# A decoder block's FFN down projection: deeper operand look-ahead, another order of its seven products, and a last product that is finished group by group

## The chip, the cores and the metric

The kernel runs on one core of a Trainium2 chip. The metric is the device time of one execution in microseconds (us); the time given for a kernel is the median of its runs.

A core has these engines, each with a queue of its own that is worked off in order: PE (matrix products, into PSUM), DVE (elementwise vector work), ACT (copies, casts, activations), POOL (here a power of small columns) and SP, which in this kernel issues all DMAs. Engines wait for each other by semaphores.

## The reference

One decoder block on x of 2048 tokens by 1024, all in float32, batch 1. The first half (attention and mLSTM mixers) is not touched. The change is in the feed-forward half:

```python
h2 = modulate(rms_norm(x, g_pre_ffn[l]), shift_f, scale_f)
ff = (jax.nn.silu(h2 @ w_ffn_gate[l]) * (h2 @ w_ffn_up[l])) @ w_ffn_down[l]
x = x + gate_f[:, None, :] * rms_norm(ff, g_post_ffn[l])
```

w_ffn_gate and w_ffn_up are 1024 x 2816, w_ffn_down is 2816 x 1024. The last product, its root-mean-square norm over 1024 columns and the residual sum are what the text below calls "down".

## The kernel before

A float32 product is made of three PE products of split operands: each operand is cast by ACT to a high half (fp32r) and DVE subtracts that from the original for the low half; high x high, high x low and low x high are summed in PSUM. Such a pair of halves for a 128 x 512 operand is a tile called `hl`; a ring of four `hl` tiles is shared by all of this (an operand part of down needs two: one of the activations, one of the weight).

The FFN is the second program of the kernel, `program2`. It works on two blocks of 1024 tokens: gate_up(0), down(0), gate_up(1), down(1). gate_up and down use a scheme of seven products in place of eight for a product of 2 x 2 quadrants. `PROD` names the operands of the seven, activation first: 11·11, 12·21, S2·T2, 22·T4, S1·T1, S3·T3, S4·22 (the S and T are sums of quadrants). Products 1, 3, 5 and 7 (index in `IN_X` = 0, 2, 4, 6) add up in one set of four PSUM tiles, `acc`, that is never cleared within a stage; products 2, 4 and 6 go to a second set of four, `mix`. The four tiles of a set are the four groups of 128 tokens.

In down(b2) a product has 11 parts along the contraction (2816 / 2 / 128), and a part is for each of the four token groups three matmuls of 512 columns: 7 x 11 x 4 x 3 = 924 matmuls of a stage.

- `load_ab` loads two parts at once, 1 MB, from the DRAM scratch `as_d` (sums of activations that gate_up stored, L1472) and from `ws_d` or w_ffn_down (L1475, L1478). Its tile is a `raw` (a pool of two) or a `big` (a pool of nine), as `raw2` counts; every second one is a `big` when `F["deep"]` is set.
- `run2` drives it: up to two loads are alive at a time, four when deep, and the operands of up to `ahead` parts (2 in down) are split (`split_unit`, L1146 on ACT, L1147 on DVE) before the part's matmuls are written.
- At the end of each product `combine` reads the PSUM tiles: after products 1, 3 and 5 a copy on ACT, after 2 and 4 one sum on DVE per token group, after 6 two sums (L1375, L1376), which complete quadrants 21 and 22. With quadrant 11 complete after product 2, 21 and 22 after 6, 12 after 7, `done` runs a chain for each token group: square and row sum on ACT (L1492), multiplication by the gain on DVE (L1494), and where both halves of a row are there the sum (L1499), the mean (L473, DVE), a power -1/2 (L476, POOL), and two scalar_tensor_tensor on DVE (L1506) with the loaded x1 rows, each followed by a store to the output.
- In down(0), seven of the nine `big` tiles hold gate_up(1)'s operands of h (`HC`), until gate_up(1) ends. The same stage also makes the next block's h by a stream, `h_combine`: x1 loads (`ob`), DVE L1245, four transposes on PE (L210), ACT L1253, and its splits and sums. A stream's steps are written between matmuls of products in `acc` only, by `tick`, where its own clock of modelled time says so.

The order in which each engine runs its instructions is set by a scheduler at build time, from the program order, the dependencies and its own costs, unless instructions are kept in program order by hand. Of the DMA semaphores eight take turns, so that a DMA may wait for the one eight before.

## Time and profile before

| quantity | value |
|---|---|
| median of 3 runs | 2745.63 us (2745.53 to 2746.5) |
| profiled execution | 2749.36 us, its span 2747.7 us |
| PE busy | 2688.8 us, 98% |
| DVE busy | 1927.2 us, 70% |
| ACT busy | 1235.1 us, 45% |
| granted clock, mean | 0.993 |
| down(0) by the trace | 1868.07 to 2098.12 us |
| gate_up(1) | to 2516.8 us |
| down(1), PE's part | to 2736.3 us |

The profile is that of one execution. Times are us from the span's start. "L1147" is a line of the kernel, "hl<-big,hl" the output tile and the inputs by their names in the program, "x4" a number of instructions in a row, and a bracket such as "[1.81 <-DVE hl L1147]" says that the engine stood idle for 1.81 us before and what ended the wait. PE's duration of one matmul (0.39 us) is longer than the distance between starts, since matmuls overlap.

### The profile page before, as it was taken

Reading aid. Unit: us, or ns where it says so; the run is one execution under the profiler, and the core shown is the slowest. Engines: PE = TensorE matmul, PEld = TensorE weight load, DVE = VectorE, ACT = ScalarE, POOL = GpSimd, SP = SyncE. Lnnn points to the kernel's source line nnn. Section 1 sums busy time; section 2 is a strip of 40 time slices with the busy share of each in tenths; the row PEclk is TensorE's granted clock in tenths of the full one; section 3 lists DMA queues with packets and bytes.
Section 4 is the critical chain, followed back from the end, with each engine's and each line's share of the span. In section 5 each row is a group of like instructions: output and inputs, shape, how many; then the busy total and the mean of one; then the engine's idle time right before and its main releaser. Section 6 shows DMA issues by size and latency. Waiting matters only on the chain.

```text
span 2747.7 us, 35099 instructions
## 1 busy us (share of the span) xinstructions
PE 2688.8 (98%) x12654; PEld 2203.2 (80%) x12654; DVE 1927.2 (70%) x3780; ACT 1235.1 (45%) x2278; POOL 238.0 (9%) x255
## 2 busy tenths in 40 slices
PE   6999999999999999999999999999999999999997
PEld 4778887788887887878887888887877888888886
DVE  7768657677776876668747777776669666666556
ACT  4543354533555345564334333334555333333444
POOL 3100121001211012110111000000001000000000
PEclk8999999999999999999999999999999999999999
DMA  7233254252453534434457444456557332326534
GB/s 230 94 113 99 92 177 131 81 154 93 149 158 105 167 116 161 163 106 147 140 201 262 152 154 173 142 188 211 199 201 248 114 102 98 111 96 238 209 132 169
DMA packets 282102, 417.32 MB, mean 152 GB/s; under 512 B 18996, under 2 KB 176312, under 8 KB 280136
## 3 DMA queue, kind: packets, MB, share of 16 engines
q1 hardware_dynamic: 281928, 415.08, 45.6%
q8 instruction: 99, 1.62, 0.2%
q14 instruction: 75, 0.61, 0.1%
HBM read 331.11 MB, written 83.92 MB: 151 GB/s over the span
## 4 chain that ended last, share of the span: by engine, by line
PE 86%; DVE 6%; DMA 4%; ACT 2%; issue 1%; SPq 0%; POOL 0%; POOLq 0%; DVEq 0%; ACTq 0%
PE acc L205 60%; PE mix L205 24%; PE mix L210 2%; DVE tm L427 1%; DMA tx<-in_x_dram 1%; DMA ob<-x 1%; DMA hc_d<-os 1%; DVE hl L1147 1%; DMA tx<-in_w_ada_dram 1%; DMA big<-in_x_dram 0%; DVE wlo L263 0%; DMA big<-in_w_ada_dram 0%; ACT hl L1146 0%; DMA w<-x 0%; ACT whi L262 0%
## 5 line engine op out<-in xcount | busy, mean ns | idle before, releaser
L262 ACT CAST whi<-raw 128x1024 fp32r<-128x1024 f32 (+1 forms) x208 | 211.8, 1019 | 425.4 <-PE acc L205 349.9
L263 DVE TENSOR_TENSOR wlo<-raw,whi 128x1024 fp32r<-128x1024 f32 (+1 forms) x208 | 252.8, 1216 | 144.6 <-ACT whi L262 142.3
L205 PE MATMUL acc<-hhi,wlo 128*128 128x512 f32 x896 | 353.9, 395 | 0.0
L205 PE MATMUL acc<-hlo,whi 128*128 128x512 f32 x896 | 352.4, 393 | 0.0
L205 PE MATMUL acc<-hhi,whi 128*128 128x512 f32 x896 | 352.1, 393 | 0.2 <-ACT whi L262 0.2
L1146 ACT CAST hl<-raw 128x512 fp32r<-128x512 f32 x309 | 185.0, 621 | 224.9 <-PE mix L205 127.6
L205 PE MATMUL acc<-hl,hl 128*128 128x512 f32 x1056 | 252.1, 396 | 8.4 <-DVE hl L1147 6.9
L205 PE MATMUL acc<-big,hl 128*128 128x512 f32 x1056 | 253.9, 389 | 0.3 <-ACT w L1368 0.3
L1147 DVE TENSOR_TENSOR hl<-raw,hl 128x512 fp32r<-128x512 f32 x309 | 206.9, 687 | 67.3 <-ACT hl L1146 65.1
L205 PEld LDWEIGHTS acc<-hl,hl 128*128 128x128 f32 x1056 | 198.4, 190 | 55.2 <-DVE hl L1147 12.2
L205 PEld LDWEIGHTS acc<-big,hl 128*128 128x128 f32 x1056 | 198.1, 188 | 41.7 <-ACT w L1368 0.7
L1147 DVE TENSOR_TENSOR hl<-big,hl 128x512 fp32r<-128x512 f32 x219 | 144.7, 687 | 84.5 <-ACT hl L1146 84.5
L1146 ACT CAST hl<-big 128x512 fp32r<-128x512 f32 x219 | 128.5, 621 | 159.2 <-PE acc L205 79.5
L205 PEld LDWEIGHTS acc<-hhi,wlo 128*128 128x128 f32 x896 | 168.4, 188 | 36.9 <-DVE tm L868 1.6
L205 PEld LDWEIGHTS acc<-hlo,whi 128*128 128x128 f32 x896 | 168.3, 188 | 36.6 <-issue 1.6
L205 PEld LDWEIGHTS acc<-hhi,whi 128*128 128x128 f32 x896 | 168.4, 188 | 34.4 <-ACT whi L262 0.6
L205 PE MATMUL mix<-big,hl 128*128 128x512 f32 x704 | 195.6, 389 | 0.0
L205 PE MATMUL mix<-hl,hl 128*128 128x512 f32 x792 | 181.1, 389 | 0.3 <-ACT hl L1146 0.3
L205 PEld LDWEIGHTS mix<-hl,hl 128*128 128x128 f32 x792 | 148.5, 188 | 31.9 <-ACT hl L1146 1.2
L205 PE MATMUL acc<-whi,big 128*128 128x512 f32 x512 | 164.7, 395 | 1.4 <-ACT whi L262 1.4
L205 PE MATMUL acc<-big,whi 128*128 128x512 f32 x512 | 157.6, 392 | 0.0
L205 PEld LDWEIGHTS mix<-big,hl 128*128 128x128 f32 x704 | 132.1, 188 | 27.4
(309 smaller groups left out, 5113.8 us busy)
## 6 DMA issues: line engine op xcount, KB each, us to landing
raw<-in_w_in_dram SPq DMA_DIRECT2D x76, 1024.0 KB
as_d<-w SPq DMA_DIRECT2D x154, 256.0 KB
raw<-in_w_ffn_up_dram SPq DMA_DIRECT2D x22, 1024.0 KB
big<-as_d SPq DMA_DIRECT2D x41, 512.0 KB
tx<-in_w_ada_dram SPq DMA_DIRECT2D x64, 256.0 KB
raw<-in_w_out_dram SPq DMA_DIRECT2D x16, 1024.0 KB
raw<-as_d SPq DMA_DIRECT2D x29, 512.0 KB
hc_d<-os SPq DMA_DIRECT2D x28, 512.0 KB
```

The source lines that it names most:

```text
L205: return T.matmul(o, lhsT=lhsT, rhs=rhs, start=start, stop=stop, skip_group_check=resumed)
L210: T.transpose(o, i, ident[:k, :k])
L262: A.copy(hv, src)
L263: eng.tensor_tensor(lv, src, hv.bitcast(F32), op=ALU.subtract)
L427: V.scalar_tensor_tensor(acc, raw[:, k, :], c_, acc, op0=ALU.mult, op1=ALU.add)
L1146: A.copy(v(hi), src)
L1147: V.tensor_tensor(v(lo), src, v(hi).bitcast(F32), op=ALU.subtract)
```

## The change

- The order of the products is 1, 4, 3, 6, 5, 2, 7 (index 0, 3, 2, 5, 4, 1, 6), and `gather` stands in place of `combine` in down: quadrant 21 is complete after product 6, the fourth to run, 22 after product 5, 11 after product 2, the sixth, and 12 last. The copies and sums of a stage are as many as before.
- `ahead` is 3 in down(0) and 4 in down(1). One part of three in down(0), and two of four in down(1), are split into a `big` tile ("roomy") in place of two `hl`.
- `F["deep"]` is a number: 2 at first, 3 from the last pair of gate_up(0) on, 4 from the end of down(0) on. That many loads are alive; with 3 every third load is a `big`, with 4 every second.
- The last four parts of product 7 in down(1) (`HELD`) are kept in four `big` tiles. Their 48 matmuls come at the end, one token group after the other, 12 for each, pinned in program order.
- `done` became a generator `chain`. In down(0) and for quadrant 12 it runs on the spot; for the other quadrants of down(1) it is run as a stream, `after`, behind the sums, and is finished ahead of the held parts.

```diff
-                if nload < len(raws) and alive < (4 if F["deep"] else 2):
+                if nload < len(raws) and alive < F["deep"]:
...
-        return big(shape) if F["deep"] and F["loads"] % 2 else raw_tile(shape)
+        return big(shape) if F["deep"] > 2 and F["loads"] % (2 if F["deep"] == 4 else 3) == 1 else raw_tile(shape)
...
+        def done(t):
+            def go(qd, y, in_psum):
+                steps = chain(t, qd, y, in_psum)
+                if in_psum:
+                    next(steps)
+                if in_psum or not last:
+                    for _ in steps:
+                        pass
+                else:
+                    behind.append(steps)
...
+        def after():
+            while True:
+                while behind:
+                    yield from behind.pop(0)
+                if F["chained"] == b2:
+                    return
+                yield 1000.0
...
+        def gather(i, ps, r, done):
+            if i == 0:
+                r["P1"] = unit()
+                A.copy(r["P1"], ps)
+            elif i == 3:
+                r["Q"] = unit()
+                A.copy(r["Q"], ps)
+            elif i == 2:
+                V.tensor_tensor(r["Q"], ps, r["Q"], op=ALU.add)
+            elif i == 5:
+                r["Z"] = unit()
+                A.copy(r["Z"], ps)
+                V.tensor_tensor(r["Q"], ps, r["Q"], op=ALU.add)
+                done("21", r["Q"], False)
+            elif i == 4:
+                V.tensor_tensor(r["Z"], ps, r["Z"], op=ALU.add)
+                done("22", r["Z"], False)
+            elif i == 1:
+                V.tensor_tensor(r["P1"], ps, r["P1"], op=ALU.add)
+                done("11", r["P1"], False)
+            else:
+                done("12", ps, True)
+
+        ahead = 4 if last else 3
...
         def make(raw, i, p, j):
+            roomy = made[0] % ahead in ((0, 2) if last else (0,))
+            made[0] += 1
+            held = last and i == 6 and p >= NP - HELD
+
             def prep():
+                if held or roomy:
+                    t = big([4, TB], F32R)
+                    return split_unit(raw.tile[:, j, :], t[:, 0, :], t[:, 1, :]) + split_unit(raw.tile[:, 2 + j, :], t[:, 2, :], t[:, 3, :])
                 return split_unit(raw.tile[:, j, :]) + split_unit(raw.tile[:, 2 + j, :])
...
+                if held:
+                    if not kept:
+                        F["chained"] = b2
+                        finish([F["after"]])
+                    kept.append(ab)
+                    if p < NP - 1:
+                        return
...
+                pin = tc.keep_in_program_order if held else lambda ins: ins
...
+                    for ah, al, bh, bl in kept if held else [ab]:
+                        pin(mm(ps, ah[:, c], bh, p == 0 and i in (0, 1, 3, 5), False, True))
+                        pin(mm(ps, ah[:, c], bl, False, False, True))
+                        pin(mm(ps, al[:, c], bh, False, p == NP - 1 and ah is ab[0], True))
...
-            pt.ahead = 2
+            pt.ahead = HELD if held else ahead
...
-        for i in range(7):
+        for i in (0, 3, 2, 5, 4, 1, 6):
```

How the instructions stand on the engines, at three places. In these rows a name carries two numbers, the tile's and the buffer's count, and rows with the same names are put together as "x3".

PE where gate_up(0) ends and down(0) begins, before: `big` operands with `acc2747` are gate_up's last parts, `acc2768` to `acc2770` belong to down's first part, and `ob2780` is what the stream transposes.

```order
L205 MATMUL acc2747_16216<-big2231_12755,hl2749_16231 128x512
L205 MATMUL acc2747_16216<-big2230_12753,hl2749_16231 128x512
L205 MATMUL acc2768_16375<-hl2761_16339,hl2760_16336 128x512
L205 MATMUL acc2769_16376<-hl2761_16339,hl2760_16336 128x512
L205 MATMUL acc2770_16377<-hl2761_16339,hl2760_16336 128x512
L205 MATMUL acc2768_16375<-hl2761_16339,hl2760_16336 128x512 x2
L205 MATMUL acc2769_16376<-hl2761_16339,hl2760_16336 128x512 x2
L205 MATMUL acc2770_16377<-hl2761_16339,hl2760_16336 128x512 x2
L210 MATMUL mix2788_16491<-ident_116,ob2780_16437 128x128 x4
L205 MATMUL acc2747_16216<-big2271_13032,hl2753_16269 128x512
```

The same place now:

```order
L205 MATMUL acc2747_16216<-big2230_12753,hl2749_16231 128x512
L210 MATMUL mix2787_16494<-ident_116,ob2779_16438 128x128 x4
L205 MATMUL acc2747_16216<-big2271_13032,hl2753_16269 128x512
L205 MATMUL acc2747_16216<-big2272_13034,hl2753_16269 128x512
L205 MATMUL acc2747_16216<-big2271_13032,hl2753_16269 128x512 x2
L205 MATMUL acc2747_16216<-big2272_13034,hl2753_16269 128x512
L205 MATMUL acc2747_16216<-big2271_13032,hl2753_16269 128x512 x2
L205 MATMUL acc2747_16216<-big2272_13034,hl2753_16269 128x512
L205 MATMUL acc2747_16216<-big2271_13032,hl2753_16269 128x512 x2
L205 MATMUL acc2747_16216<-big2272_13034,hl2753_16269 128x512
L205 MATMUL acc2747_16216<-big2271_13032,hl2753_16269 128x512
L205 MATMUL acc2768_16377<-big2758_16314 128x512
```

The nine matmuls of down's first part moved behind the transposes and gate_up's last part; that part's operands are now in a `big` tile, `big2758`.

DVE in down(1) where the sixth product to run ends, before: `mix3735` and the next three are that product's PSUM tiles, `w` the quadrants' sums, and L1147 the splits of coming parts.

```order
L1147 TENSOR_TENSOR hl3763_22811<-big3748_22694,hl3763_22811 128x512
L1375 TENSOR_TENSOR w3664_22141<-mix3735_22615,w3664_22141 128x512
L1376 TENSOR_TENSOR w3728_22589<-mix3735_22615,w3728_22589 128x512
L1375 TENSOR_TENSOR w3665_22146<-mix3736_22616,w3665_22146 128x512
L1376 TENSOR_TENSOR w3729_22594<-mix3736_22616,w3729_22594 128x512
L1375 TENSOR_TENSOR w3666_22151<-mix3737_22617,w3666_22151 128x512
L1376 TENSOR_TENSOR w3730_22599<-mix3737_22617,w3730_22599 128x512
L1375 TENSOR_TENSOR w3667_22156<-mix3738_22618,w3667_22156 128x512
L1376 TENSOR_TENSOR w3731_22604<-mix3738_22618,w3731_22604 128x512
L1147 TENSOR_TENSOR hl3796_22918<-big3748_22694,hl3796_22918 128x512
```

And now, after the sixth product to run (product 2):

```order
L1147 TENSOR_TENSOR big3746_22928<-raw3720_22763,big3746_22928 128x512
L1553 TENSOR_TENSOR w3564_21659<-mix3685_22581,w3564_21659 128x512
L1147 TENSOR_TENSOR big3747_22945<-raw3720_22763,big3747_22945 128x512
L1147 TENSOR_TENSOR big3748_22962<-big3729_22814,big3748_22962 128x512
L1553 TENSOR_TENSOR w3565_21664<-mix3686_22582,w3565_21664 128x512
L1147 TENSOR_TENSOR big3748_22962<-big3729_22814,big3748_22962 128x512
L1553 TENSOR_TENSOR w3566_21669<-mix3687_22583,w3566_21669 128x512
L1147 TENSOR_TENSOR big3749_22979<-big3729_22814,big3749_22979 128x512
L1553 TENSOR_TENSOR w3567_21674<-mix3688_22584,w3567_21674 128x512
L1147 TENSOR_TENSOR big3749_22979<-big3729_22814,big3749_22979 128x512
```

The eight sums in a row became four, with splits of parts far ahead (`big3746` to `big3749`, which hold the last parts of the last product) between them.

PE's last matmuls before, the last part of the last product:

```order
L205 MATMUL acc3563_21475<-hl3817_23089,hl3816_23086 128x512
L205 MATMUL acc3564_21476<-hl3817_23089,hl3816_23086 128x512
L205 MATMUL acc3565_21477<-hl3817_23089,hl3816_23086 128x512
L205 MATMUL acc3566_21478<-hl3817_23089,hl3816_23086 128x512
L205 MATMUL acc3563_21475<-hl3817_23089,hl3816_23086 128x512 x2
L205 MATMUL acc3564_21476<-hl3817_23089,hl3816_23086 128x512 x2
L205 MATMUL acc3565_21477<-hl3817_23089,hl3816_23086 128x512 x2
L205 MATMUL acc3566_21478<-hl3817_23089,hl3816_23086 128x512 x2
```

And now, from the second token group on:

```order
L205 MATMUL acc3541_21463<-big3749_22979 128x512 x3
L205 MATMUL acc3541_21463<-big3750_22996 128x512 x3
L205 MATMUL acc3542_21464<-big3747_22945 128x512 x3
L205 MATMUL acc3542_21464<-big3748_22962 128x512 x3
L205 MATMUL acc3542_21464<-big3749_22979 128x512 x3
L205 MATMUL acc3542_21464<-big3750_22996 128x512 x3
L205 MATMUL acc3543_21465<-big3747_22945 128x512 x3
L205 MATMUL acc3543_21465<-big3748_22962 128x512 x3
L205 MATMUL acc3543_21465<-big3749_22979 128x512 x3
L205 MATMUL acc3543_21465<-big3750_22996 128x512 x3
```

The four token groups ended within two matmuls of each other; now each ends twelve matmuls after the one before.

More of the change, by code (lines that the diff above doesn't have):

```diff
@@ L1130, in decoder_block @@
     HC = {}
-    F = {"rest": [], "loads": 0, "deep": False}
+    F = {"rest": [], "loads": 0, "deep": 2}
     as_d = [tc.dram_tile([P, 7, NP, TB], F32, name=f"as_d{i}") for i in range(NB2)]
@@ L1455, in gate_up @@
                 if p + 1 == NP:
-                    yield lambda: F.update(deep=True)
+                    yield lambda: F.update(deep=3)
             yield from up[3:]
@@ L1483, in down, with chain @@
         ss = {}
+        kept = []
+        HELD = 4
         def done(t):
             def go(qd, y, in_psum):
+                steps = chain(t, qd, y, in_psum)
[6 more added lines that the diff above has]
+                    behind.append(steps)
+            return go
+        behind = []
+        def after():
[5 more added lines that the diff above has]
+                yield 1000.0
+        def chain(t, qd, y, in_psum):
                 row, half = int(qd[0]) - 1, int(qd[1]) - 1
@@ L1495, in go @@
                 Y[tok, half] = o
+                yield 1500.0
                 if (tok, 1 - half) not in Y:
@@ L1524, in mms, with first @@
                     c = slice(t * P, (t + 1) * P)
-                    mm(ps, ah[:, c], bh, p == 0 and i in (0, 1, 3, 5), False, True)
-                    mm(ps, ah[:, c], bl, False, False, True)
-                    mm(ps, al[:, c], bh, False, p == NP - 1, True)
-                    yield
+                    for ah, al, bh, bl in kept if held else [ab]:
+                        pin(mm(ps, ah[:, c], bh, p == 0 and i in (0, 1, 3, 5), False, True))
+                        pin(mm(ps, ah[:, c], bl, False, False, True))
+                        pin(mm(ps, al[:, c], bh, False, p == NP - 1 and ah is ab[0], True))
+                        yield
                     if p == NP - 1:
-                        combine(i, ps, R[t], unit, done(t))
+                        gather(i, ps, R[t], done(t))
             pt = Part(raw, prep, mms, weave=i in IN_X)
-            pt.ahead = 2
+            pt.ahead = HELD if held else ahead
             return pt
+        def first():
+            F["chained"] = None
+            F["after"] = spawn(after())
+        if last:
+            yield first
         if not last:
@@ L1546, in down @@
                     yield make(raw, i, p0 + j, j)
+        if not last:
+            yield lambda: F.update(deep=4)
+        yield lambda: F.update(chained=b2)
     def placed(name):
```

4 lines of the change are left out of this document (2 added, 2 removed).

## The prediction

> **What bounds the kernel.** I read the page first, for the share of each engine and the chain that ended last.
>
> ```profile
> PE 2688.8 (98%) x12654; PEld 2203.2 (80%) x12654; DVE 1927.2 (70%) x3780; ACT 1235.1 (45%) x2278; POOL 238.0 (9%) x255
> PE 86%; DVE 6%; DMA 4%; ACT 2%; issue 1%; SPq 0%; POOL 0%; POOLq 0%; DVEq 0%; ACTq 0%
> ```
>
> PE is busy for 98% of the span, and 86% of the chain that ended last is PE. No product is added or removed by the change, so PE's 98% stays. What can be won is what PE loses in the two down stages and what comes after its last matmul. Next I read windows, one for each stage: down of the first 1024 tokens, the boundary after it, the second gate/up stage, the second down stage, and the rest behind the last matmul. The columns are the length, then busy us and count on PE, PEld, DVE, ACT, POOL, then the granted clock, the DMA share and GB/s.
>
> ```profile
> 1868.07:2098.12 230.05, 223.37 (x991) 180.62 (x990) 158.66 (x261) 126.34 (x232) 4.57 (x4) 0.99 0.65 219
> 2098.12:2120.00 21.88, 21.35 (x93) 16.93 (x92) 20.34 (x41) 10.59 (x23) 3.00 (x4) 1.00 0.86 293
> 2120.00:2516.80 396.80, 396.80 (x1752) 328.67 (x1751) 271.98 (x438) 143.71 (x251) 0.00 (x0) 1.00 0.32 106
> 2516.80:2736.30 219.50, 215.74 (x937) 176.13 (x935) 125.20 (x205) 101.72 (x194) 2.81 (x4) 0.99 0.55 196
> 2736.30:2747.70 11.40, 0.00 (x0) 0.00 (x0) 7.86 (x20) 1.08 (x4) 3.04 (x4) 0.70 0.49 184
> ```
>
> The third row is PE with no loss: 396.80 us for 1752 matmuls, 0.2265 us each. By this price the first down stage, with 931 such matmuls and 60 small transposes (0.35 us for four, by the starts 1870.12 and 1870.47 below: 5.3 us), needs 210.9 + 5.3 = 216.2 us and takes 230.05: **13.9 us lost**. The second down stage needs 937 x 0.2265 = 212.2 us and takes 219.5: **7.3 us lost**. The boundary needs 93 x 0.2265 = 21.1 us of 21.88: 0.8 us. The last row is **11.4 us** with no matmul at all. Together 33.4 us; nothing else in this program can be shortened by the change.
>
> The waits of PE in each of the two down stages, and what single stalls look like in the timeline:
>
> ```profile
> PE acc L205 <- DVE hl L1147: 4.0, 4, 1.8
> PE mix L210 <- DVE ob L1245: 1.3, 2, 0.7
> PE acc L205 <- ACT hl L1146: 0.7, 1, 0.7
> PE mix L205 <- ACT hl L1146: 0.7, 2, 0.3
> PE acc L205 <- DVE hl L1147: 2.9, 2, 2.3
> 1870.12 0.60 PE L210 MATMUL mix<-ident,ob 128*128 128x128 f32 x4
> 1870.47 3.01 PE L205 MATMUL acc<-big,hl 128*128 128x512 f32 x12
> 1874.19 3.70 PE L205 MATMUL acc<-hl,hl 128*128 128x512 f32 x15 [0.71 <-ACT hl L1146]
> 1880.68 3.70 PE L205 MATMUL acc<-hl,hl 128*128 128x512 f32 x15 [1.44 <-DVE hl L1147]
> 2065.30 1.18 PE L205 MATMUL acc<-hl,hl 128*128 128x512 f32 x4
> 2068.30 6.42 PE L205 MATMUL acc<-hl,hl 128*128 128x512 f32 x20 [1.81 <-DVE hl L1147]
> 2700.72 3.79 PE L205 MATMUL acc<-hl,hl 128*128 128x512 f32 x16
> 2706.80 15.86 PE L205 MATMUL acc<-hl,hl 128*128 128x512 f32 x60 [2.29 <-DVE hl L1147]
> 2723.30 12.99 PE L205 MATMUL acc<-hl,hl 128*128 128x512 f32 x56 [0.65 <-DVE hl L1147]
> ```
>
> Two things are to be seen. First, PE waits for the split parts (hl, line 1147), mostly after the sixth product (2066 and 2704). Second, what a stall costs beyond itself. After 1.44 us idle, 15 matmuls took 3.70 us, or (3.70 - 0.39) / 14 = 0.236 each. After 1.81 us idle 20 took 6.42, or 0.317 each: (0.317 - 0.2265) x 19 = 1.7 us more. After 2.29 us idle 60 took 15.86: (15.86 - 0.39) - 59 x 0.2265 = 2.1 us more. So somewhere between 1.44 and 1.81 us idle a stall starts to cost about another 1.7 us; the granted clock of that stage is 0.99, of the others 1.00. [...]
>
> **The stalls after the sixth product, and the ring of splits.**
>
> ```profile
> 2059.70 1.14 ACT L1146 CAST hl<-big 128x512 fp32r<-128x512 f32 x2 [1.58 <-PE mix L205]
> 2062.42 0.62 ACT L1146 CAST hl<-big 128x512 fp32r<-128x512 f32 x1 [1.58 <-PE mix L205]
> 2061.57 0.68 DVE L1375 TENSOR_TENSOR w<-mix,w 128x512 f32<-128x512 f32 x1
> 2065.76 0.68 DVE L1376 TENSOR_TENSOR w<-mix,w 128x512 f32<-128x512 f32 x1
> 2066.36 0.68 DVE L1147 TENSOR_TENSOR hl<-big,hl 128x512 fp32r<-128x512 f32 x1
> 2067.56 0.68 DVE L1147 TENSOR_TENSOR hl<-big,hl 128x512 fp32r<-128x512 f32 x1
> ```
>
> ACT's casts wait for PE to release the part two back; that is the ring of two. The cast at 2062.42 was ready, but its subtraction stood behind eight sums on DVE (first at 2061.57, last at 2065.76, 0.60 apart), and the second subtraction of the part ended at 2068.2, where PE starts. The change does two things to this. The burst becomes four sums, 2.4 us shorter, since each product now closes one or two sums per token group. And the ring grows from two parts to three in the first down stage (one in three in a big tile) and to four in the second (two in four), which lets the preparation start one or two parts, 2.72 or 5.44 us (12 matmuls x 0.2265 each), earlier. Against a stall of 2.0 us (2068.30 minus the end of four matmuls from 2065.30, 3.00 - 4 x 0.2265 = 2.1) that is 2.4 + 2.72 = 5.1 us and more: it goes in both stages, with its slow matmuls. What is late next is the transposes of the stream of the next block's h.
>
> First down stage, term by term, by the four rows of its waits: nine waits, 6.7 us idle, and each costs 0.16 us more by the starts (2068.30 - 2065.30 - 4 x 0.2265 = 2.1 for 1.81 idle is the largest). Sixth product: 2.1 + 1.7 = 3.8, to 0. Start (0.71, 1.44, and about 0.25 of the two short waits that are left of DVE's four, 4.0 - 1.44 - 1.81 = 0.75): 2.9, see below. Other hl waits, the other short one, 0.5, and one of ACT's two on mix, 0.35: 1.1 by the starts, to 0.3 by the longer ring. The transposes' two waits, 1.3 idle: 1.6. Their x1 load and its sum on DVE are not changed, so I leave them, bounded below by 0 (splits ready earlier leave DVE freer) and above by 4 (DVE now has chain parts after products four and five, where it had none). One wait at the stage's end, 0.5, stays. These make 9.9 of 13.9; the other 4.0 are restarts that are not called waits, such as the 14 x 0.01 after 1880.68, and of those I keep half, since they go with the stalls.
>
> **The start of the first down stage** is moved to the worse. Before, nine matmuls of down's first part ran at 1868.07 to 1870.12, ahead of the transposes. In the new order they do not: the first part goes into a big tile, whose place comes free only when the sums of the last w_down pair are written, and PE meets the transposes at 1868.07.
>
> ```profile
> 1868.07 2.21 PE L205 MATMUL acc<-hl,hl 128*128 128x512 f32 x9
> 1862.83 0.75 SPq L1240 DMA_DIRECT2D ob<-x  x1
> 1869.22 0.69 DVE L1245 TENSOR_TENSOR ob<-ob,rx 128x512 f32<-128x512 f32 x1 [1.72 <-DMA ob<-x]
> 1867.53 0.32 SPq L1427 DMA_DIRECT2D as_d<-w  x1
> 1870.43 0.32 SPq L1472 DMA_DIRECT2D big<-as_d  x1
> ```
>
> The x1 load that these transposes need lets DVE's sum start at 1869.22 and end at 1869.9, so PE would wait from 1868.3 to 1870.1: about 1.8 us idle, on the edge of the two rows above. I take half of the 1.7 us: 1.8 + 0.8 = 2.6 us. The big tile's place: the load at 1870.43 into the same place waited for those writes, so the first part is split from there on (two casts and two subtractions, 1.14 + 1.3 us, to 1872.9), while PE has twelve matmuls of the gate/up stage until 1873.2. This hides, with 0.3 us to spare; if it does not, 1 to 2 us. The 1.6 us before 1880.68 goes by the ring of three. So 2.9 becomes 3.0 with 0.4 for the small one, between 2 and 5.
>
> Sum of the stage: start 3.0 + transposes 1.6 + hl 0.3 + end 0.5 + restarts 2.0 = 7.4 of 13.9: **-6.5 us** (bounds -12 and 0). The boundary's 0.8 stays, since the order of the gate/up stage there is the same but for one more sum of a raw tile in front.
>
> **Second down stage.** The stall of 2.29 us (2.4 by starts) with its 2.1 us goes: -4.5. The 0.65 before 2723.30 (0.8 by starts) goes, since those parts are among the four held in big tiles long before. The wait at its first part for ACT's hl (0.7 idle, 0.9 by starts) is the same edge as before and stays. That makes 6.2; of the other 1.1, restarts again, I keep 0.5. So 7.3 becomes 1.4: **-5.9 us** (bounds -7.3 and -3, the latter if the start gets a wait of 3 us).
>
> The four chains of the stage, for quadrants 21, 22 and 11, move behind as a stream. They are the same instructions, and DVE is busy 125.20 of 219.50 us, so 94 us are free to hold them; if DVE's order put them together the price is the burst seen above, 2.1 us.
>
> **The tail.** Before, the last product's last part ran over all four token groups, each group's last matmul 0.45 us or so after the other, so four chains ended at once.
>
> ```profile
> 2734.96 0.60 ACT L1492 ACTIVATE w<-acc 128x512 f32<-128x512 f32 x1 [2.94 <-PE acc L205]
> 2735.46 0.19 ACT L1492 ACTIVATION_READ_ACCUMULATOR w<-acc 128x1 f32 x1
> 2735.68 0.69 DVE L1494 TENSOR_TENSOR w<-acc,gg_f 128x512 f32<-128x512 f32 x1 [2.85 <-ACT w L1492]
> 2737.02 0.14 DVE L473 TENSOR_SCALAR ms<-ss 128x1 f32<-128x1 f32 x1
> 2737.31 0.55 POOL L476 TENSOR_TENSOR rs<-ms,nhalf 128x1 f32<-128x1 f32 x1 [13.66 <-DVE ms L473]
> 2737.90 1.42 DVE L1506 SCALAR_TENSOR_TENSOR w<-w,rs,w 128x512 f32<-128x512 f32 x2
> 2743.19 1.41 DVE L1506 SCALAR_TENSOR_TENSOR w<-w,rs,w 128x512 f32<-128x512 f32 x2 [0.44 <-POOL rs L476]
> ```
>
> One chain alone is: square at 0 (2734.96), multiplication at 0.72 (2735.68), sum 0.61 later, mean at 1.40; mean to POOL 0.29 and to the first scalar_tensor_tensor 0.88 (2737.02 to 2737.90), so 2.28; two of them 1.41: 3.69. From the end of the last, 2744.60, to the span's end, 2747.7, it is 3.1 us, the store. With four parts held and the groups run one after another, the last matmul of a group is 48 matmuls / 4 = 12 x 0.2265 = 2.72 us after the one before, and a chain on DVE is 0.68 + 0.15 + 0.14 + 1.41 = 2.4 us of work: three chains are over or nearly so when the last starts. Tail: 0.03 + 3.69 + 3.1 = 6.8, and 0.2 for the rest of the third chain: 7.0 of 11.4: **-4.4 us** (bounds -4.6 and -3.0; the x1 loads of the last group stand on SP behind stores of the second and could be late by some 0.7, and POOL's powers in the rows take 0.55 to 1.0).
>
> **Sum.** -6.5 - 5.9 - 4.4 = -16.8 us. The profiled run took 2749.36 us (span 2747.7 and 1.7 around it), 3.7 above the median of the three runs, 2745.63; the losses are differences within it, so I take them off the median: **2728.8 us**. On the page of the changed kernel that would be a span near 2731.
>
> **Rivals.**
>
> *DVE eats the first stage's gain.* DVE is busy 158.66 of 230.05 us there, and with the stage at 224 us it would be 71% on average; but the chains of 22 and 21 with their eight scalar_tensor_tensor now fall behind product five, beside the stream of the next h. If that product lacks 3 us of DVE and the start costs 5, the stage gains 0 to 2. For it: the two transposes' waits on DVE. Against: the longer ring rides over a burst. Then -5.9 - 4.4 = -10.3: **2735.3**.
>
> *All waits go.* The start is hidden, the transposes are on time: 13.9 + 0.8 + 7.3 + 4.4 = 26.4 at the most, **2719.2**. Against: the x1 load at 1869.22.
>
> *Slower: loads late.* In the first down stage three pairs are alive where four were. A pair of parts lasts 5.44 us; with three alive, one being split, and splits 2.72 us further ahead, a load must land within 2 x 5.44 - 2.72 = 8.2 us of its issue, where it had 16.3. The stage moves 219 GB/s at a DMA share of 0.65, and the load of 256 KB behind the writes at 1862.83 took until 1869.22, 6.4 us; in front of the loads on SP stand stores and x1 loads. If each of the 42 pairs came 0.4 us past 8.2, 42 x 0.4 = 17 us would eat all of the above; at 1 us, 42 - 10.3 makes +32: **2777**. It decides from a mean landing of 8.6 us. Against: 6.4 is the longest landing in the rows above.
>
> *The change doesn't do what it says in the first stage.* Seven of nine big tiles hold the operands of the other stage; if the ring of three waits for places, the stalls there stay and a further 5 to 8 us come (each of seven products once a stall of 1 us): -10.3 + 7 = -3: **2742.6**, no difference.
>
> **Chances.** My forecast 0.55 (2722 to 2733), DVE eats it 0.21, all waits go 0.12, no difference 0.07, slower 0.05. Changes of under 0.2% (5.5 us) cannot be told from none. The range reaches from the second rival's end, 2719, to 2738, which is the first rival's 2735.3 with the 3 us by which a start of 5 us and a late store in the tail may exceed it; outside lie the last two cases, 0.12, and the edges of the others, some 0.05. Faster 0.55 + 0.21 + 0.12 = 0.88, same 0.07, slower 0.05.
>
> **What would show it.** In the changed kernel's windows PE's loss should be near 7 us in the first down stage and 1 to 2 in the second, no hl wait of over 1 us after the products' ends, the square of the last group within 0.1 us of the last matmul, and 7 us behind it. The first transposes of the stage should show a wait of some 1.8 us. A DVE that is busy above 95% in slices of the first down stage, or DVE and ACT waiting on "DMA raw" or "DMA big" there, would prove the first or third rival.

## The result, and the profile after

The changed kernel's median is 2733.11 us (2731.47 to 2733.79, six runs) against 2745.91 us for the kernel before (2745.34 to 2748.88, six runs): ratio 0.995, 95% interval 0.994 to 0.9959, so 12.8 us less, faster by more than 0.2%. The forecast was 2728.8 us, with a range of 2719 to 2738: right in sign and in its range, 4.3 us too low. The profiled execution took 2731.47 us, its span 2729.5.

The page of the changed kernel, the row of busy times:

```profile
PE 2678.8 (98%) x12654; PEld 2198.4 (81%) x12654; DVE 1924.5 (71%) x3780; ACT 1234.2 (45%) x2278; POOL 243.1 (9%) x255
```

PE was busy for 10 us less at the same 12654 instructions. The windows of the changed kernel, cut at the corresponding places: first down stage, boundary, second gate/up stage, second down stage, and the rest behind the last matmul (length; busy us and count on PE, PEld, DVE, ACT, POOL; clock, DMA share, GB/s).

```profile
1864.63:2093.00 228.37, 223.73 (x1010) 183.48 (x1008) 160.74 (x265) 128.43 (x237) 7.84 (x4) 1.00 0.67 221
2093.00:2115.00 22.00, 20.65 (x90) 16.64 (x90) 21.88 (x43) 9.89 (x20) 3.07 (x4) 1.00 0.85 290
2115.00:2505.68 390.68, 390.68 (x1726) 323.48 (x1724) 266.88 (x430) 142.96 (x249) 0.00 (x0) 1.00 0.32 103
2505.68:2721.80 216.12, 215.34 (x949) 177.66 (x947) 129.28 (x217) 100.50 (x194) 4.06 (x7) 1.00 0.61 209
2721.80:2729.50 7.70, 0.01 (x1) 0.00 (x0) 3.65 (x7) 0.69 (x2) 0.80 (x2) 0.81 0.67 230
```

By the working of the prediction (0.2265 us a matmul, 5.3 us for 60 transposes): the first stage has 950 matmuls, 215.2 + 5.3 = 220.5 of 228.37 us: 7.9 lost, where it was 13.9. The boundary: 90 x 0.2265 = 20.4 of 22.0: 1.6, where it was 0.8. The second stage: 949 x 0.2265 = 214.9 of 216.12: 1.2, where it was 7.3. The tail: 7.7, where it was 11.4. Together -15.0 us.

What PE waits for in the changed kernel, in the first stage with its boundary, and (last row) in the second:

```profile
PE mix L210 <- DVE ob L1245: 3.4, 2, 1.9
PE mix L205 <- DVE hl L1147: 1.2, 3, 0.8
PE acc L205 <- ACT w L1362: 0.7, 1, 0.7
PE mix L205 <- ACT hl L1146: 0.6, 1, 0.6
PE acc L205 <- DVE w L1422: 0.8, 1, 0.8
```

The waits for hl after the sums are gone: 4.0 and 2.9 us became 1.2 and none. More than half of the idle time that is left is the transposes, twice, in the timeline of PE (the last row is the pinned end, 60 matmuls with no gap):

```profile
1866.60 0.66 PE L210 MATMUL mix<-ident,ob 128*128 128x128 f32 x4 [1.58 <-DVE ob L1245]
2084.99 0.66 PE L210 MATMUL mix<-ident,ob 128*128 128x128 f32 x4 [1.86 <-DVE ob L1245]
2708.05 13.76 PE L205 MATMUL acc<-big 128*128 128x512 f32 x60
```

**Why 15.0 in the profiles and 12.8 in the medians.** The two programs are the same up to the end of the first gate/up stage, and yet the profiles differ there. To set this aside, all profiles below are cut at the same PE instructions by count: 8870, shortly before the first down stage, 9970 behind its boundary, 11690 shortly before the second down stage, and the last, 12653. Instruction 8870 starts at 1864.42 us in the first profile of before and at 1861.21 in that of the changed kernel; in three more profiles of the two it lies between 1860.39 and 1864.49. So 3.2 of the 18.2 us between the two spans are variation of a part that both share. From 8870 to the end it is 883.3 and 882.3 us in two profiles of before, and 868.3, 867.8 and 867.3 in three of the changed kernel: 15.0 us less between their means. The three comparisons of medians say 12.8, 13.6 and 14.8, and the interval of the first ratio alone is 11 to 16 us.

### The profile page after: what moved, and what is told of

Its sections match the earlier page's. It is cut to its first block, busy times and chain, and to the rows that moved or that the text cites. A ratio compares the mean times of both kernels' runs of the same rounds, so it can differ in the third digit from the quotient of the medians.

```text
span 2729.5 us, 35015 instructions
## 1 busy us (share of the span) xinstructions
PE 2678.8 (98%) x12654; PEld 2198.4 (81%) x12654; DVE 1924.5 (71%) x3780; ACT 1234.2 (45%) x2278; POOL 243.1 (9%) x255
## 4 chain that ended last, share of the span: by engine, by line
PE 86%; DVE 6%; DMA 4%; issue 2%; ACT 1%; POOL 0%; SPq 0%; DVEq 0%; POOLq 0%; ACTq 0%
PE acc L205 61%; PE mix L205 23%; PE mix L210 2%; DMA ob<-x 1%; DVE tm L427 1%; DMA hc_d<-os 1%; DMA tx<-in_w_ada_dram 1%; DVE hl L1147 1%; DMA tx<-in_x_dram 1%; DMA big<-in_x_dram 0%; DVE wlo L263 0%; DMA raw<-in_w_ffn_down_dram 0%; DVE w L1532 0%; DMA big<-in_w_ada_dram 0%; DVE big L1147 0%
## 5 line engine op out<-in xcount | busy, mean ns | idle before, releaser
L1146 ACT CAST hl<-raw 128x512 fp32r<-128x512 f32 x274 | 165.4, 622 | 184.3 <-PE mix L205 110.1
L1147 DVE TENSOR_TENSOR hl<-raw,hl 128x512 fp32r<-128x512 f32 x274 | 183.7, 685 | 41.6 <-ACT hl L1146 39.3
L476 POOL TENSOR_TENSOR rs<-ms,nhalf 128x1 f32<-128x1 f32 (+1 forms) x40 | 32.8, 823 | 1397.0 <-DVE ms L473 1395.7
L205 PE MATMUL acc<-wlo,hhi 128*128 128x512 f32 (+1 forms) x384 | 139.2, 367 | 1.1 <-DVE wlo L263 0.6
L205 PE MATMUL acc<-whi,hhi 128*128 128x512 f32 (+1 forms) x384 | 130.7, 367 | 8.8 <-ACT hhi L509 6.9
L205 PE MATMUL acc<-hl,hl 128*128 128x512 f32 x564 | 135.7, 391 | 0.0
L205 PE MATMUL acc<-whi,hlo 128*128 128x512 f32 (+1 forms) x384 | 135.1, 361 | 0.3 <-POOL hlo L512 0.3
L205 PE MATMUL mix<-hc,hl 128*128 128x512 f32 x528 | 134.0, 389 | 0.0
```

The lines of the kernel that those rows point to most:

```text
L205: return T.matmul(o, lhsT=lhsT, rhs=rhs, start=start, stop=stop, skip_group_check=resumed)
L476: G.tensor_tensor(r[:, :n], ms[:, :n], nhalf[:, :n], op=ALU.pow)
L1146: A.copy(v(hi), src)
L1147: V.tensor_tensor(v(lo), src, v(hi).bitcast(F32), op=ALU.subtract)
```

## The experiments

Twelve more runs were made, of eleven kernels, the kernels before and after among them. This table is worked out from the traces: the time between the same two instructions of PE, less 0.2265 us for each matmul of 512 columns and 0.089 for each transpose in between (it agrees with the windows above to 0.6 us). "Tail" is from the start of the last matmul to the span's end. The medians in a row are of one chip; rows of different chips are not to be compared with each other but by the column from 8870.

| kernel | first down stage and boundary, lost us | second down stage, lost us | tail, us | from 8870 to the end, us | median, us | before beside it, us |
|---|---|---|---|---|---|---|
| before | 15.2 | 7.3 | 11.8 | 883.3 | 2745.9 | |
| before_again | 15.2 | 6.4 | 11.8 | 882.3 | 2747.1 | 2747.0 |
| after | 10.0 | 1.2 | 8.1 | 868.3 | 2733.1 | 2745.9 |
| after_again | 9.5 | 1.2 | 8.1 | 867.8 | 2733.4 | 2747.0 |
| after_third | 8.9 | 1.2 | 8.1 | 867.3 | 2731.7 | 2746.5 |
| ring2 | 14.8 | 7.3 | 8.1 | 879.2 | 2745.2 | 2747.0 |
| ring2_held1 | 14.4 | 5.2 | 11.1 | 879.7 | 2744.3 | 2747.3 |
| old_order | 14.4 | 1.7 | 13.4 | 878.4 | 2742.6 | 2747.0 |
| before_held | 15.6 | 12.9 | 8.1 | 885.6 | 2748.5 | 2747.3 |
| held1 | 9.0 | 1.2 | 11.1 | 870.3 | 2735.5 | 2747.3 |
| held5 | 10.1 | 1.2 | 10.2 | 870.5 | 2735.4 | 2747.3 |
| spot | 9.5 | 1.2 | 8.1 | 867.9 | 2734.2 | 2747.9 |
| best1 | 9.4 | 1.2 | 7.4 | 866.9 | 2731.2 | 2747.9 |
| best2 | 8.6 | 1.2 | 7.3 | 866.2 | 2731.5 | 2746.5 |

### The kernel before, once more (before_again)

No edit.

> The kernel before, unchanged, for a second profile of it. The first profiled run lay 3.7 us above its median; the changed kernel's lay 1.6 below. Theory: the losses of the two down stages are set by the order and come again as they were (13.9 and 7.3 us, tail 11.4), and the difference between the profiled runs, 18.2 us against 12.8 of the medians, is the start of the program, which both kernels share and where the two profiles differ by 3.2 us. Rival: the losses themselves vary from run to run, the two stalls of about 2 us and their slow matmuls (1.7 and 2.1 us) above all; then this profile shows 3 to 5 us less of them. Time 2745.6 to 2746.5 in both.

Ratio 0.9999 (0.999 to 1.0008). The losses came again: 15.2 in the first stage, 6.4 where there were 7.3 in the second, tail 11.8. But how they came was not the same. PE after the sums of the sixth product, timeline, first stage and second:

```profile
2064.09 5.26 PE L205 MATMUL acc<-hl,hl 128*128 128x512 f32 x20 [1.83 <-DVE hl L1147]
2074.15 3.02 PE L205 MATMUL acc<-hl,hl 128*128 128x512 f32 x12 [0.71 <-DVE hl L1147]
2702.75 8.93 PE L205 MATMUL acc<-hl,hl 128*128 128x512 f32 x36 [2.29 <-DVE hl L1147]
2712.22 13.02 PE L205 MATMUL acc<-hl,hl 128*128 128x512 f32 x53 [0.54 <-DVE hl L1147]
```

The waits are as long as in the first profile (1.83 and 2.29 us; there 1.81 and 2.29), but no slow matmuls follow: 20 in 5.26 us, where the first profile had 20 in 6.42. And nothing was won by it: a wait of 0.71 us came some 10 us later, and the stage lost the same 15.2. The slow matmuls had been filling time in which DVE was behind anyway. So the prediction's 1.7 us for "a stall of this length" was neither tied to the length nor a cost of its own in the first stage. In the second, the same difference is 0.9 us of 7.3.

### The changed kernel, twice more (after_again, after_third)

No edit.

> The changed kernel as it is, to stand beside the next two on the same chip and for a second profile: 2732 to 2734; losses of 7.9 us in the first down stage, 1.6 at its boundary, 1.2 in the second, a tail of 7.7, each within 1 us if they are set by the order.

> The changed kernel as it is, for the same chip: 2733 to 2734; stages as in its two profiles, and the wait of PE at the last transposes of the first stage, 2.0 us in one profile and 1.2 in the other, somewhere in 0.6 to 2.0, since it depends on when the next stage's first weight lands.

Ratios 0.995 (0.9938 to 0.9963) and 0.9946 (0.9934 to 0.9959). Second stage and tail came the same to 0.03 us. In the first stage one thing moves most: the wait at the last transposes, 2.0, 1.2 and 0.5 us by the starts, the last just under the 0.6 to 2.0 expected. after_third's median, 2731.7 us, is also a little under what was expected. The wait at the first transposes was 1.7 to 2.2 us in all three.

### The look-ahead taken back (ring2)

```diff
-        ahead = 4 if last else 3
+        ahead = 2
...
-            roomy = made[0] % ahead in ((0, 2) if last else (0,))
+            roomy = False
```

> The changed kernel with a look-ahead of two parts in both down stages and no part in a big tile but the four that are held; order of products, spread sums, stream and held end as changed. Theory, as in the prediction (the longer ring and the smaller burst each do half): the stalls after the sums come back in part, 2 to 4 us in each stage, time 2737 to 2741. Rival 1, the ring alone carries it: 4 to 7 us in each stage, 2742 to 2746. Rival 2, the spread sums alone carry it: no stall of over 1 us in the second stage, within 2 us of the changed kernel. With two parts the nine matmuls of down's first part stand ahead of the first transposes again, so that wait of 1.6 us should go in any case.

2745.24 us, ratio 0.9991 (0.9982 to 1.0): nearly all of the gain but the tail's was gone, more than the theory had it. The time is that of rival 1, but the second stage lost its 7.3 us mostly for another reason than the sums. The waits of PE in the first stage, and then the timeline of ACT and PE in the second around the end of the sixth product to run:

```profile
PE mix L210 <- DVE ob L1245: 3.7, 2, 3.2
PE mix L205 <- DVE hl L1147: 2.6, 4, 1.0
PE mix L205 <- ACT hl L1146: 1.1, 2, 0.7
```

```profile
2699.11 0.62 ACT L1146 CAST big<-raw 128x512 fp32r<-128x512 f32 x1 [2.01 <-DMA raw<-as_d]
2699.64 2.18 ACT L1146 CAST big<-big 128x512 fp32r<-128x512 f32 x4
2701.72 0.61 ACT L1146 CAST hl<-big 128x512 fp32r<-128x512 f32 x1
2703.52 8.72 PE L205 MATMUL acc<-hl,hl 128*128 128x512 f32 x30 [2.15 <-ACT hl L1146]
```

In the first stage the waits for hl are back (3.7 us and a short one), and the second transposes wait 3.2 us: the load of their x1 rows went out at 1868.12, behind a big load at 1867.28 that had to wait for its place (in the changed kernel, at 1864.68). The 19 matmuls that follow take 6.18 us, 1.7 more than at 0.2265 us apart, so this one place makes some 5 of the stage's 14.8 us. In the second stage ACT waits 2.01 us for the operands of the held parts, casts five of them, and only then comes to the cast for the next part, at 2701.72; PE stands for 2.15 us and then goes slow: 30 matmuls in 8.72 us, where 30 took 6.96 us just before (from 2691.68). With a look-ahead of two the held end itself makes a stall. The spread sums did not prevent it.

### The same without the held end (ring2_held1)

```diff
 # ring2, and
-        HELD = 4
+        HELD = 1
...
-            pt.ahead = HELD if held else ahead
+            pt.ahead = ahead
```

> Look-ahead of two in both stages and one held part: of the change the new order with its spread sums, the stream and the loads are left. Theory: the stall of 2.3 us with slow matmuls, which the second stage showed with look-ahead 2 and four held parts, was made by the held casts; without them the four sums (2.4 us, ring slack 0.8) cost 1.5 to 2 us once and some 0.7 a few times: loss 3 to 5 us, tail 11 to 12. Rival 1, the ring of two cannot carry even four sums: 6 to 7 us as before. Rival 2, spread sums carry the stage: under 2 us.

2744.34 us, ratio 0.9989 (0.9979 to 0.9998); the second stage lost 5.2 us, just above the theory's 3 to 5, but not where it had it. DVE and PE, timeline:

```profile
2685.68 0.75 DVE L1532 SCALAR_TENSOR_TENSOR w<-w,rs,w 128x512 f32<-128x512 f32 x1 [1.16 <-DMA w<-x]
2687.69 12.99 PE L205 MATMUL mix<-hl,hl 128*128 128x512 f32 x56 [1.89 <-DVE hl L1147]
2700.51 27.84 PE L205 MATMUL acc<-hl,hl 128*128 128x512 f32 x120
```

The four sums at the product's end cost nothing: 120 matmuls run from 2700.51 without a gap. The loss lies 15 us earlier, where a scalar_tensor_tensor of the chains waits 1.16 us for its x1 rows on DVE, the third such wait in a row, and the next splits stand behind it (PE 1.89 us). So with a ring of two the smaller burst alone is enough against the stall after the sums, but not against the chains.

### The old order under the new look-ahead (old_order)

```diff
-        for i in (0, 3, 2, 5, 4, 1, 6):
+        for i in range(7):
...
 # gather: after product 6 (index 5) both sums, and done("21") and done("22"), as combine had it
```

> The changed kernel with the seven products in their old order, 1 to 7, and the old sums (two for each token group after the sixth product, quadrants 21 and 22 complete at once); look-ahead of 3 and 4, stream and held end as changed. Theory: a ring of four rides over a burst of eight sums (4.8 us against 2 x 2.72 of lead), so the second stage loses 1 to 2 us as changed; in the first, with three, 1 to 3 us come back; time 2734 to 2737. Rival, the spread sums carry it: stalls of 2 us with slow matmuls after the sixth product in both stages, 2740 to 2742.

2742.55 us, ratio 0.9983 (0.9974 to 0.9991), past the theory's 2734 to 2737, and the rival had the wrong reason: there is no stall after the sixth product. The second stage lost 1.7 us, 0.5 more than as changed, so a ring of four does ride over eight sums. In the first stage, with three, PE waits for no hl at all. What is lost is at the ends. PE, DVE and SP at the end of the first stage, and DVE in the tail:

```profile
2094.94 1.12 PE L210 MATMUL mix<-ident,ob 128*128 128x128 f32 x4 [4.95 <-DVE ob L1245]
2094.20 0.69 DVE L1245 TENSOR_TENSOR ob<-ob,rx 128x512 f32<-128x512 f32 x1 [1.96 <-DMA ob<-x]
2080.13 2.96 SPq L1533 DMA_DIRECT2D out_dram<-w  x4
2084.39 2.83 SPq L1240 DMA_DIRECT2D ob<-x  x1
2719.12 2.15 DVE L1532 SCALAR_TENSOR_TENSOR w<-w,rs,w 128x512 f32<-128x512 f32 x3 [2.84 <-DMA w<-x]
```

Both quadrants' chains fall behind the sixth product, four of their stores and two weight loads stand on SP in front of the load for the last transposes, and that goes out at 2084.39 only; DVE's sum starts at 2094.20 and PE has stood for 4.95 us. The four transposes then take 1.12 us and the matmul behind them 0.78 us, where four transposes without a wait (at 2083.07) took 0.60 us and a matmul takes 0.39 us. In the second stage the chains of 21 and 22 are not over when the first held group ends, and DVE waits 2.84 us for x1 rows: the tail is 13.4 us, longer than before the change. So beside the longer ring the new order pays by what it does to the chains' DMAs, not by the smaller burst of sums.

### The held end alone (before_held), one held part (held1), five (held5)

```diff
 # before_held: before.py, with held, kept, pin and HELD = 4 as in the change, and nothing else of it
 # held1: the changed kernel with
-        HELD = 4
+        HELD = 1
...
-            pt.ahead = HELD if held else ahead
+            pt.ahead = ahead
...
 # held5: the changed kernel with
-        HELD = 4
+        HELD = 5
```

> The kernel before with the held end alone: four parts of the last product in big tiles, group by group, pinned; old order, look-ahead 2, chains on the spot. Theory: the tail's gain comes by itself, 11.8 to 8.1 or so, and the second stage keeps its 6.4 to 7.3 us of loss: 2743 to 2744. Rival, from the look-ahead of two with a held end, where four casts for the held parts stood ahead of the next hl cast and PE lost 2.3 us and slow matmuls: the held casts add a stall of 2 to 4 us here, and the time stays near before, 2745 to 2748.

> The changed kernel with one held part in place of four (and the usual look-ahead for it), so that the four token groups end three matmuls apart, 0.68 us, as good as together. Theory: the gain behind the last matmul is the held end alone; the time from the start of the last matmul to the span's end, 8.1 us in both profiles of the changed kernel and 11.8 in both of before, goes back to 11 to 12, the stages stay, time 2736 to 2738. Rival: the stream and the early chains had already shortened the tail; then 9 to 10 and 2734 to 2735.

> The changed kernel with five held parts. In its profile a chain takes 3.00 us on DVE (0.73 of it waiting for POOL) and the groups come 2.72 us apart, so each starts 0.28 us later than the one before and the last multiplication stands 0.8 us behind its square. Theory: with five parts the groups come 3.40 us apart, DVE keeps up, and the 8.1 us become 7.3; time 0.8 less, which only the profile can tell. Rival: the last group waits for its x1 rows or the stores set the end: 8.1 stays.

before_held: 2748.52 us, ratio 1.0009 (1.0 to 1.0018). The tail's gain comes whole (8.1 us), and the second stage gives it back with interest, 12.9 us lost. Its waits of PE in that stage:

```profile
PE acc L205 <- DVE hl L1147: 4.2, 3, 2.9
PE acc L205 <- ACT hl L1146: 2.8, 2, 2.1
```

The rival held, beyond its upper end: the stage lost 5.6 to 6.5 us more than in the two profiles of before, where 2 to 4 were expected, with held casts and eight sums in front of the next hl and two parts of look-ahead.

held1: 2735.49 us, ratio 0.9954 (0.9938 to 0.9971), a little under the time of its theory; stages as changed, tail 11.1, so 3.0 of the tail's 3.7 us are the held end, as the theory had it; its 11.1 is still 0.7 less than before's, which was not followed up.

held5: 2735.4 us, ratio 0.9956 (0.9942 to 0.9971), a miss: the tail is 10.2. DVE and SP:

```profile
2718.83 0.76 DVE L1532 SCALAR_TENSOR_TENSOR w<-w,rs,w 128x512 f32<-128x512 f32 x1 [2.48 <-DMA w<-x]
2714.84 0.43 SPq L1530 DMA_DIRECT2D w<-x  x1
2723.34 0.75 DVE L1532 SCALAR_TENSOR_TENSOR w<-w,rs,w 128x512 f32<-128x512 f32 x1 [1.74 <-DMA w<-x]
```

The groups came slower, as meant, but the x1 loads stand on SP behind the stores of the group before, and DVE waits for them, 2.48 and 1.74 us. So this could not tell whether DVE's drift was the tail's cost; best1 does.

### The chains on the spot (spot)

```diff
-                if in_psum or not last:
+                if True:
```

> The changed kernel with the chains of quadrants 21, 22 and 11 in the second down stage run on the spot behind their sums, not as a stream. Theory: with four parts of look-ahead the stage can carry them (it lost 1.7 us even with eight sums in a burst), so it loses 1.2 to 2.5 us and the tail stays 8.1: time within 1.5 us of the changed kernel. Rival, the stream is needed because the scalar_tensor_tensor wait for x1 rows on DVE ahead of the splits, as they did with look-ahead 2 (waits of 0.4 to 1.2 us, and 2.1 us lost by PE): loss of 4 us or more, 2737 and up.

2734.15 us, ratio 0.9948 (0.9933 to 0.9963); second stage 1.2 us, tail 8.1 and 867.9 us from 8870, as changed. Its only wait of PE in the second stage:

```profile
PE acc L205 <- DVE w L1422: 0.8, 1, 0.8
```

With the new order and the ring of four, the stream that holds the chains back brings nothing that these runs can tell.

### Three repairs (best1), two of them (best2)

```diff
 # best1 and best2
-        made = [0]
+        made = [0 if last else 1]
...
-        HELD = 4
+        HELD = 5
...
+                        for t in range(NT):
+                            for h2 in range(2):
+                                xr = pre[t, h2] = unit()
+                                nc.sync.dma_start(xr, x1[b2 * 2][t * P:(t + 1) * P, h2 * TB:(h2 + 1) * TB])
 # the chain of quadrant 12 takes these rows in place of loads of its own
...
 # best1 alone: with deep = 3, a big tile for the loads with F["loads"] % 3 == 2
```

> The changed kernel with three repairs, each to be read in its own stretch of the profile. (1) First part of the first down stage back in the hl ring, so that nine matmuls cover the wait for the first transposes, with the x1 load of the second ones still ahead of the big load: the 1.7 to 2.0 us lost there become under 0.5; rival: the next wait (second transposes) takes their place, 1 us or more. (2) The loads of the first stage that go to a big tile moved by one, so that the next gate/up stage's first weight goes to a big tile: if DVE's wait of 4.3 us for that weight, ahead of the sum for the last transposes, came from the raw tile being free too late, the 0.7 to 2.0 us lost there go; rival: the load itself is late on SP and it stays. (3) Five held parts and the x1 rows of quadrant 12 loaded ahead of them: with the rows there, the tail of 8.1 us becomes 7.0 to 7.4, by the drift of 0.28 us for each group; rival: 8 or more, the tail is set by something else. Time 2729 to 2731 if all three hold, 2733 if none.

> The repairs that held, without the moved loads: first part of the first down stage in the hl ring, five held parts with their x1 rows loaded ahead. The stage's start loses under 0.5 in place of 1.7 to 2.0, the tail is 7.35 in place of 8.1. Theory: the wait of 1.6 us inside the first stage that came with the moved loads was theirs, so it is gone here: together 2 to 2.5 us under the changed kernel on the same chip, 2730 to 2731. Rival: DVE is full in that stretch, and what the start gains is lost in the next wait whatever the loads: 0.8 to 1 us under the changed kernel, from the tail alone.

best1 2731.15 us, ratio 0.9941 (0.9929 to 0.9954); best2 2731.45 us, ratio 0.9943 (0.9929 to 0.9956), beside 2731.7 for the changed kernel on the same chip: no difference that can be measured. By the column from 8870 best2 is 1.1 to 2.2 us shorter than the changed kernel's three profiles. PE and DVE of best2: the start, the end of the first stage, the tail.

```profile
1871.79 0.66 PE L210 MATMUL mix<-ident,ob 128*128 128x128 f32 x4 [0.20 <-DVE ob L1245]
2092.39 2.57 PE L205 MATMUL mix<-hc,hl 128*128 128x512 f32 x10 [1.54 <-DVE hl L1147]
2081.21 0.69 DVE L1315 TENSOR_TENSOR w<-raw 128x512 f32<-128x512 f32 x1 [4.22 <-DMA raw<-in_w_ffn_gate_dram]
2722.49 0.69 DVE L1519 TENSOR_TENSOR w<-acc,gg_f 128x512 f32<-128x512 f32 x1 [0.31 <-ACT w L1517]
2724.17 1.41 DVE L1535 SCALAR_TENSOR_TENSOR w<-w,rs,w 128x512 f32<-128x512 f32 x2 [0.73 <-POOL rs L476]
```

The tail's repair held: with the x1 rows there and the groups 3.4 us apart, the last multiplication waits for its square only (2722.49, idle before it), and the tail is 7.3. The start's repair held in its place, 0.2 us idle for 1.6 to 2.0, and did little for the stage, which lost 8.6 us where the changed kernel's profile on the same chip lost 8.9: PE came earlier to the stage's end, where DVE still waits 4.2 us for the next stage's first weight, and a new wait of 1.54 us for hl stands at 2092.39. So best2 came out nearer to its rival than to its theory's 2 to 2.5 us. The moved loads of best1 did not bring that weight earlier (DVE waited 4.39 us there) and added a wait of 1.4 us inside the stage; best2 without them has only 0.2 us there.

## Why the prediction was right, and where its terms were off

- **First down stage, -6.5 forecast, -6.0 by the windows** (13.9 to 7.9; 7.0 to 8.1 in three profiles by the table's cut without the boundary). Right in its sum. The stall after the sums went, as said, and each of the two causes was enough to end it: with the longer ring and the old eight sums PE waits for no hl (old_order), and with the old ring and four sums no wait is left behind the sixth product, the longest elsewhere being 1.0 us (ring2). But neither alone wins the stage, which with its boundary loses 14.4 and 14.8 us in these two, above all at transposes that wait for their x1 rows (4.95 and 3.2 us). The other hl waits, 0.3 forecast, were 1.2 us idle. The 1.7 us for "slow matmuls" in it were no term of their own (before_again): the stage loses as much without them.
- **The start, 3.0 forecast.** The wait that the new order brings was there, 1.58 us idle by the timeline and 1.7 to 2.2 by the starts in three profiles, for the x1 rows as forecast. The 0.8 us for slow matmuls were not: after 1.58 us, and after 1.86 at the last transposes, none followed; the granted clock is 1.00 in the 4 us from the start of either, with 20 and 19 instructions on PE. The prediction's edge, between 1.44 and 1.81 us idle, was its author's estimate from two stalls of one profile, and the later profiles do not bear it out: 1.83 us in before_again and 1.86 here had no slow matmuls behind them.
- **Transposes and boundary, 1.6 and 0.8 forecast, unchanged.** This is the first step that failed, though the 1.6 came out about right: two waits of 0.8 us by the starts became one at the last transposes, of 2.0, 1.2 and 0.5 us in the three profiles. That the size fits is luck, since the cause is another. The prediction wrote that the order at the boundary is "the same but for one more sum of a raw tile in front", and costed that at nothing. SP and DVE of the changed kernel there, and then (last three rows) of the kernel before:

```profile
2076.40 0.38 SPq L1389 DMA_DIRECT2D raw<-in_w_ffn_gate_dram  x1
2081.84 0.69 DVE L1315 TENSOR_TENSOR w<-raw 128x512 f32<-128x512 f32 x1 [4.26 <-DMA raw<-in_w_ffn_gate_dram]
2084.25 0.68 DVE L1245 TENSOR_TENSOR ob<-ob,rx 128x512 f32<-128x512 f32 x1
2081.34 0.38 SPq L1389 DMA_DIRECT2D big<-in_w_ffn_gate_dram  x1
2088.90 0.69 DVE L1315 TENSOR_TENSOR w<-big 128x512 f32<-128x512 f32 x1
2090.11 0.68 DVE L1245 TENSOR_TENSOR ob<-ob,rx 128x512 f32<-128x512 f32 x1
```

In the changed kernel the sum L1315 waits 4.26 us for the next stage's first weight, and the sum for the last transposes (L1245, at 2084.25) stands behind it in DVE's queue; PE waits 1.86 us for it. In the kernel before L1315 stood ahead of L1245 too, but DVE came to it 7.6 us after the load of the weight went out (2081.34 to 2088.90) and waited for nothing; now DVE is there 1.2 us after (2076.40 to 2081.84 - 4.26 = 2077.58). Two more sums of the next stage (L1316 and L1322, at 2083.05 and 2083.65) now stand between as well, 1.2 us. This is read from the traces; no run changed it alone, and in best1, where the load went to another tile, it landed no sooner after its issue. The boundary itself went from 0.8 to 1.6 us by two other waits (ACT's copy 0.7, hl 0.6), whose cause was not followed up. A wait in front of work that PE needs is a term of the sum, even where the order of the instructions is nearly the same.
- **Second stage, -5.9 forecast, -6.1 measured.** Right in size. A wait at its first part (0.8 us) stayed, as said, but it is now for a sum on DVE (L1422) and not for ACT's hl, so that this term is right by luck. old_order shows that the longer ring is enough against the stall, with all eight sums (1.7 us lost). ring2_held1 shows that four sums are enough too, but with the ring of two the stage still loses 5.2 us, most of it beside the chains.
- **Tail, -4.4 forecast, -3.7 measured.** The second step that failed, by its size: the prediction took a chain on DVE as "2.4 us of work", shorter than the 2.72 us between groups. Queue time, not work, was what counted. ACT and DVE of the changed kernel at the end:

```profile
2721.91 0.60 ACT L1516 ACTIVATE w<-acc 128x512 f32<-128x512 f32 x1 [2.09 <-PE acc L205]
2720.41 0.68 DVE L1518 TENSOR_TENSOR w<-acc,gg_f 128x512 f32<-128x512 f32 x1
2722.08 1.42 DVE L1532 SCALAR_TENSOR_TENSOR w<-w,rs,w 128x512 f32<-128x512 f32 x2 [0.73 <-POOL rs L476]
2723.41 0.68 DVE L1518 TENSOR_TENSOR w<-acc,gg_f 128x512 f32<-128x512 f32 x1
2725.08 1.42 DVE L1532 SCALAR_TENSOR_TENSOR w<-w,rs,w 128x512 f32<-128x512 f32 x2 [0.73 <-POOL rs L476]
```

A chain occupies DVE for 3.00 us (2720.41 to 2723.41), since DVE stands still for 0.73 us while POOL computes the power. Each group drifts by 0.28 us; the last multiplication could start 0.72 us after its square, 2722.63, and starts at 2723.41. That is 0.8 us where 0.2 was forecast, and best1 and best2 got it back, by five held parts with the x1 rows loaded ahead; five held parts alone (held5) did not.
- **The rivals.** "DVE eats it" did not come in the changed kernel: no wait of over 0.8 us for hl. "Loads late" came in one place, the weight at the boundary, and for up to 2 us of PE, not for each pair. Its sign, DVE waiting on "DMA raw", did show there, so the sign was too wide. That all waits go was excluded by the x1 load, as argued. "No difference" did not come: the first stage with its boundary lost 10.0 us where it had lost 15.2. The number of loads alive, three in place of four in the first stage, was varied by no run.
- **The 4.3 us** by which the forecast was low are 1.8 of these terms (15.0 for 16.8: first stage 0.5, boundary 0.8, tail 0.7, less 0.2 of the second stage), 2.2 between the profiles' 15.0 and the medians' 12.8, and 0.3 by which the second median of before was higher than the first. The 2.2 are not explained by any one term; the profiles of before differ by 1 us from 8870 on and the later medians gave 13.6 and 14.8, so it may be no more than the spread of the runs.

## What to carry to other kernels

Look at what a waiting instruction has behind it on its own queue: three of the things that moved the time here (the weight's sum, with its wait of 4.26 us, ahead of the transposes' sum; the held casts ahead of the next split, 2.15 us of PE in ring2; stores ahead of x1 loads, 2.48 and 1.74 us of DVE in held5) are waits of an in-order queue, and none shows in a share of busy time (PE 98% before and after, DVE 70% and 71%). The longer look-ahead is what made another rearrangement pay here: with two parts of look-ahead the held end cost the second stage 5.6 to 6.5 us in the old order (before_held against before) and 2.2 in the new (ring2 against ring2_held1), and with four nothing (held1). And take a stage's loss as a whole before pricing the pieces of it: a piece that goes (slow matmuls, a wait at the start) can come back as the next wait (0.71 us in before_again, 1.54 us in best2).

## What the runs showed of the hardware

A wait of PE of about the same length was followed by slow matmuls in one run and not in another of the same kernel: 1.81 us idle with 20 matmuls in 6.42 us, 1.83 us with 20 in 5.26; 2.29 us with 60 in 15.86 us and, in the other, 36 in 8.93. The granted clock shows the same. The first 4 us after the stall in the first stage, in the first profile of before and in before_again (columns as in the windows above):

```profile
2068.30:2072.30 4.00, 4.00 (x11) 3.17 (x12) 4.00 (x9) 0.37 (x2) 0.00 (x0) 0.57 0.91 307
2064.10:2068.10 4.00, 3.88 (x16) 2.89 (x17) 4.00 (x9) 1.22 (x3) 0.00 (x0) 1.00 0.92 280
```

The granted clock is 0.57 with 11 matmuls and 1.00 with 16. No run here varied the gap alone, so what decides is open.
